# A hybrid decoder layer: an SSM norm's scaling as four jobs, with new places for sample matmuls, norm matmuls, PSUM banks and weight splits

## The chip, the cores and the metric

One core of one Trainium2 chip runs the kernel. The metric is the device time of one execution in microseconds (us), as the median of a kernel's runs.

## The reference

One decoder layer acts on 1024 prompt tokens (with 16 learned tokens ahead of them, 1040 columns) and on 8 sample tokens, so 1048 columns in the mixing part and 1032 after it. The model width is 1024, and everything is fp32.

```python
h += 0.5 * SwiGLU_1(rmsnorm(h))             # width 2816
u  = rmsnorm(h) @ w_in                      # q, f, v, g of 4 HGRN2 heads; z, x, B, C, dt of the SSM
# HGRN2, per head, chunkwise: S_t = diag(f_t) S_{t-1} + k_t v_t^T ; o_t = S_t^T q_t
#   then rmsnorm per head, times silu(u_g)
# SSM (Mamba-2): h_t = exp(dt_t A) h_{t-1} + dt_t x_t B_t^T ; y_t = h_t C_t + D x_t
#   then y * silu(z), rmsnorm over each of 2 groups of 256
h += concat(hgrn_out, ssm_out) @ w_out
h += 0.5 * SwiGLU_2(rmsnorm(h))
y  = rmsnorm(h)                             # the states are outputs too
```

Each of the 8 sample tokens has a state of its own for every head: the state is read, updated by one step, written out, and multiplied with the token's q.

## The kernel before

**Layout.** Activations lie transposed: a tile holds 128 features by all columns. A product has fp32 accuracy by three matmuls of rounded parts (`mm3`, L163 to L165: high by high, high by low, low by high). These three lines hold most of the program; a triple of them on 128 features and one column range is called a k-step here. Splitting a tile into the two parts takes one copy on ACT and one subtraction on DVE (L462 and L466 for FFN weights, L346 and L352 for FFN operands, L157 and L158 for w_in and w_out).

**PSUM.** Four banks ("mis", `K.psm()`) serve small things, and four ("acc") serve the wide products: two pairs in the FFNs (`K.psum2()`), and four single banks elsewhere (`K.psum()`). `K.banks(n)` closes and reopens the acc pool; `down` calls it ahead of its last product.

**FFNs.** Each runs seven products in place of eight per block of four weight tiles, in the manner of Strassen; the numbers 1 to 7 name them. `Blocks` makes the operands of one column half (`scaled` is ACT L335, `sum_` is DVE L341, `cast` is ACT L346, `low` is DVE L352), `Left` the weights (`sum_`, then `split` = `hi` L462 and `lo` L466). `pair` computes a gate and up tile and evacuates each product in `post`: 1 by an ACT copy L674, 6 by DVE L676 (which needs the copy), 2 by ACT L678, 5 by DVE L683 (which needs L676), 7 by L685. `first2` lists the order of the second FFN's first pair, whose operands are made while its first products run: `before(S, n, ...)` puts work ahead of step n. In an FFN the order of PE, DVE, ACT and SP is this written one. `down` ends an FFN; its evacuation is DVE L932.

**The mixing part.** The four HGRN2 heads run one after another (`hgrn_scan`). A head goes through levels m = 1, 2, 4, ..., 64 with small matmuls (L1767, and L1758 for m = 32 and 64), then transposes, chunk states (L1835), outputs (L1854 to L1861) and, last, the output of the 8 sample tokens, L1864: the 128x128 state against one column of q. Between these come the wide w_in products: `fill(n)` issues n k-steps, and every `fill.period`-th k-step pops one entry of the list `fill.jobs`. `samples` updates four states at a time (L1717 on ACT, L1718 on DVE) in levels 2 and 16. In this part only PE's order is the written one; ACT, DVE and SP are ordered by a scheduler with a cost model.

**Norms.** `ssm_norm` squares and sums, forms 1 / rms and multiplies two tiles of 128x1032 by it (L1625); group 0 runs after head 0, with z0 projected, group 1 at the end of the part. `hgrn_out` normalizes a head: ACT squares (L1875), a matmul against ones sums over partitions (L1890, head 3 only), `rstd_wide` makes 1 / rms (L194 to L204), DVE multiplies (L1881). Head 3's `hgrn_out` and all of `out_proj` stand after the written order and are ordered by the scheduler on every engine. `out_proj` runs four times: part 1 on column half 0 is the pass whose `after2` feeds the second FFN's norm `nf2` (squares on ACT L229, sums on POOL L230, the matmul L237, and so on). Its DVE addition of a bank to h is L1912.

## Time and profile before

| what | value |
|---|---|
| three runs | 1952.58, 1956.12, 1958.87 us; median 1956.12 |
| the profiled execution's own time | 1959.24 us |
| its span, first to last instruction | 1957.5 us |
| mean granted clock of TensorE | 0.993 |
| DMA | 260.59 MB, mean 133 GB/s |

The profile is of one execution; the 1.74 us between its time and its span lie around the program. Engines are PE (TensorE), DVE (VectorE), ACT (ScalarE), POOL (GpSimd) and SP. A row of a table by windows gives a stretch in us from the span's start, its length, the busy time and number of instructions of each engine, the granted clock of PE as a share of full speed, the busy share of the DMA engines and GB/s. A row of a timeline gives start, length, engine, line, operation, tiles and shape, and in brackets the idle time ahead of it with what ended it. fp32 matmuls appear in the trace as two records each.

### The profile page before, as it was taken

How to read it: one execution, taken by the hardware profiler on the slowest of the kernel's cores; microseconds unless marked ns; L12 is line 12 of the kernel's file. 1: busy time of each engine (PE TensorE's matmuls, PEld its weight loads, DVE VectorE, ACT ScalarE, POOL GpSimd, SP SyncE). 2: the span in 40 equal slices, each digit the busy share in tenths (PEclk: the TensorE clock that was granted, in tenths of full speed). 3: DMA queues.
4: the chain of work that ended last, by engine and by line, in shares of the span. 5: the costliest groups of instructions: out<-in, count | busy, mean ns of one | idle time of the engine just before them, and what ended most of it. 6: DMA issues, size and time to landing. Idle time of an engine off the chain costs nothing.

```text
span 1957.5 us, 41043 instructions
## 1 busy us (share of the span) xinstructions
PE 1917.1 (98%) x16569; PEld 1883.5 (96%) x16569; DVE 1532.7 (78%) x2783; ACT 850.3 (43%) x1632; POOL 91.5 (5%) x155
## 2 busy tenths in 40 slices
PE   7999999999999999999999999999999999999997
PEld 6999999999999999999999999999999999999997
DVE  7788888888788867576765657888888888878965
ACT  7533233333533644466644535742332323354353
POOL 4000000000000410000000001200000000000000
PEclk9999999999999999999999999999999999999999
DMA  7223333335977551221641454224332333587862
GB/s 222 77 88 109 93 99 105 100 97 161 283 234 251 158 159 51 66 87 44 177 122 52 124 172 135 77 82 120 92 109 87 103 104 104 161 245 233 271 194 77
DMA packets 324646, 260.59 MB, mean 133 GB/s; under 512 B 17824, under 2 KB 299680, under 8 KB 324448
## 3 DMA queue, kind: packets, MB, share of 16 engines
q1 hardware_dynamic: 324216, 257.92, 43.5%
q8 instruction: 131, 2.15, 0.5%
q14 instruction: 59, 0.48, 0.1%
q0 software_dynamic: 224, 0.04, 0.0%
q10 hardware_dynamic: 16, 0.00, 0.0%
HBM read 192.90 MB, written 65.07 MB: 132 GB/s over the span
## 4 chain that ended last, share of the span: by engine, by line
PE 86%; DVE 7%; DMA 2%; ACT 2%; issue 1%; SPq 0%; POOL 0%; DVEq 0%; ACTq 0%; POOLq 0%
PE acc L163 26%; PE acc L165 25%; PE acc L164 25%; PE mis L163 1%; PE mis L165 1%; PE mis L164 1%; DVE u L352 1%; DVE ws L466 1%; DMA s<-in_x_prompt_dram 1%; DMA r<-in_w_ffn_up_dram 1%; DVE r L458 1%; PE mis L1767 1%; DMA s<-cumd 1%; PE mis L1835 0%; DVE t L669 0%
## 5 line engine op out<-in xcount | busy, mean ns | idle before, releaser
L163 PE MATMUL acc<-u,ws 128*128 128x258 f32 (+3 forms) x4248 | 1243.1, 293 | 7.5 <-DVE t L683 2.5
L164 PE MATMUL acc<-u,ws 128*128 128x258 f32 (+3 forms) x4248 | 1233.2, 290 | 4.4 <-DVE u L352 4.0
L165 PE MATMUL acc<-u,ws 128*128 128x258 f32 (+3 forms) x4248 | 1232.6, 290 | 3.3 <-DVE ws L466 3.3
L163 PEld LDWEIGHTS acc<-u,ws 128*128 128x128 f32 x4248 | 805.1, 190 | 12.9 <-issue 3.6
L164 PEld LDWEIGHTS acc<-u,ws 128*128 128x128 f32 x4248 | 807.5, 190 | 6.9 <-DVE u L352 5.0
L165 PEld LDWEIGHTS acc<-u,ws 128*128 128x128 f32 x4248 | 804.9, 189 | 4.7 <-DVE ws L466 4.6
L466 DVE TENSOR_TENSOR ws<-r,ws 128x512 fp32r<-128x512 f32 x276 | 190.9, 693 | 75.0 <-ACT ws L462 74.9
L462 ACT CAST ws<-r 128x512 fp32r<-128x512 f32 x276 | 160.1, 615 | 12.9 <-ACT ws L462 7.7
L458 DVE TENSOR_TENSOR r<-r,r 128x512 f32<-128x512 f32 x176 | 120.9, 689 | 4.8 <-DMA r<-in_w_ffn_up_dram 3.3
L681 ACT ACTIVATE t<-t 128x516 f32<-128x516 f32 (+1 forms) x41 | 26.2, 639 | 213.3 <-DVE t L669 213.3
L712 ACT ACTIVATE t<-t 128x524 f32<-128x524 f32 (+1 forms) x47 | 29.9, 639 | 196.3 <-DVE t L669 196.3
L846 DVE TENSOR_TENSOR u<-u,u 128x1048 fp32r<-128x1048 f32 (+3 forms) x84 | 97.0, 1157 | 5.5 <-ACT u L842 5.5
L669 DVE TENSOR_TENSOR t<-t,u 128x524 f32<-128x524 f32 (+1 forms) x135 | 92.9, 697 | 2.9
L158 DVE TENSOR_TENSOR ws<-r,ws 128x512 fp32r<-128x512 f32 x88 | 60.6, 699 | 42.2 <-ACT ws L157 41.9
L230 POOL TENSOR_TENSOR t<-t,t 128x262 f32<-128x262 f32 (+1 forms) x56 | 54.4, 982 | 812.5 <-ACT t L229 708.5
L903 ACT CAST ws<-u 128x512 fp32r<-128x512 f32 (+1 forms) x72 | 42.2, 586 | 102.2 <-DVE u L898 92.1
L842 ACT CAST u<-u 128x1048 fp32r<-128x1048 f32 (+3 forms) x84 | 82.9, 989 | 0.0
L932 DVE SCALAR_TENSOR_TENSOR s<-acc,s 128x524 f32<-128x524 f32 (+3 forms) x88 | 54.6, 643 | 31.7 <-PE acc L165 31.4
L903 ACT CAST ws<-r 128x512 fp32r<-128x512 f32 (+1 forms) x84 | 47.9, 582 | 70.8 <-DVE r L898 29.5
L908 DVE TENSOR_TENSOR ws<-r,ws 128x512 fp32r<-128x512 f32 (+1 forms) x84 | 57.4, 693 | 23.2 <-ACT ws L903 23.1
L157 ACT CAST ws<-r 128x512 fp32r<-128x512 f32 x88 | 53.9, 617 | 36.5 <-PE acc L165 30.6
L908 DVE TENSOR_TENSOR ws<-u,ws 128x512 fp32r<-128x512 f32 (+1 forms) x72 | 47.4, 658 | 26.5 <-ACT ws L903 26.5
(435 smaller groups left out, 2290.7 us busy)
## 6 DMA issues: line engine op xcount, KB each, us to landing
r<-in_w_ffn_down_dram SPq DMA_DIRECT2D x128, 256.0 KB
hd<-s SPq DMA_DIRECT2D x93, 258.0 KB
r<-in_w_ffn_gate_dram SPq DMA_DIRECT2D x88, 256.0 KB
r<-in_w_ffn_up_dram SPq DMA_DIRECT2D x88, 256.0 KB
hd<-s SPq DMA_DIRECT2D x77, 262.0 KB
u<-hd SPq DMA_DIRECT2D x36, 516.0 KB
u<-hd SPq DMA_DIRECT2D x28, 524.0 KB
r<-in_w_in_dram SPq DMA_DIRECT2D x56, 256.0 KB
```

What stands on the lines that cost most here:

```text
L158: self.nc.vector.tensor_sub(lo, src, hi.bitcast(F32))
L163: mm(ps, whi, xhi, start=first, stop=False, skip_group_check=more)
L164: mm(ps, whi, xlo, start=False, stop=False, skip_group_check=more)
L165: mm(ps, wlo, xhi, start=False, stop=last, skip_group_check=more)
L458: self.K.nc.vector.tensor_tensor(self.raw[p], self.raw[x], self.raw[y], op)
L462: self.K.nc.scalar.copy(self.w[p][:, : self.n * P], self.raw[p])
L466: self.K.nc.vector.tensor_sub(t[:, 512 : 512 + w], self.raw[p], t[:, :w].bitcast(F32))
L669: nc.vector.tensor_mul(t, t if src is None else src, spread.lanes(i, cs))
L842: K.nc.scalar.copy(hi, lo.bitcast(F32))
L846: K.nc.vector.tensor_sub(lo, lo.bitcast(F32), hi.bitcast(F32))
L903: nc.scalar.copy(w[p, j, g][:, : n * P], src)
L908: nc.vector.tensor_sub(t[:, 512 : 512 + n * P], box[0], t[:, : n * P].bitcast(F32))
```

## The change

1. **SSM norm.** `ssm_norm` returns its two multiplications as four functions of half a row each (128x516). Group 0's become entries of `fill.jobs`, with the spills of the two tiles as entries behind them; group 1's run at once.
2. **Sample outputs.** `hgrn_scan` issues the 8 matmuls of the sample tokens in two groups of four, in levels m = 32 and m = 64, each group into a mis bank of its own, which an ACT copy empties into a small SBUF tile `os8`. The last piece of a head's output, 24 columns before, becomes 16 columns in PSUM and 8 in `os8`.
3. **Head 3's norm.** `hgrn_out` takes mis banks for its sums, not acc banks.
4. **The norm of the second FFN, half 0.** Two `nf2.end(q)` at the end of `out_proj`'s part 1 become one `begin_half(0)` and one `finish` within the next pass.
5. **`down`.** The first block of the last product takes a mis bank.
6. **`first2`.** The products' order 1, 5, 2, 6, 7, 3, 4 becomes 1, 5, 6, 2, 7, 3, 4; the splits of weights 7 and 3 move from ahead of the first step into steps 1 to 3; `scaled` can be issued in pieces of its four rows.

```diff
-    def scaled(self, h, wcol, ps):
+    def scaled(self, h, wcol, ps, ks=range(4)):
...
-            t = self.new(p)
-            for k in range(4):
+            t = self.new(p) if 0 in ks else self.b[p]
+            for k in ks:
...
-                                box.append(K.psum()[:, :K.Q])
+                                box.append((K.psum() if c or j else K.psm())[:, :K.Q])
...
-    for i, y in enumerate((ya, yb)):
-        nc.vector.scalar_tensor_tensor(y, y, K.pc["ssm_norm"][:, 2 * g + i : 2 * g + i + 1], r, ALU.mult, ALU.mult)
+    def scale(i, cs):
+        y = (ya, yb)[i][:, cs]
+        nc.vector.scalar_tensor_tensor(y, y, K.pc["ssm_norm"][:, 2 * g + i : 2 * g + i + 1], r[:, cs], ALU.mult, ALU.mult)
+
+    return [lambda i=i, cs=cs: scale(i, cs) for i in range(2) for cs in (slice(0, TO // 2), slice(TO // 2, TO))]
...
+    os8 = small("os8", P, NS)
+
+    def outputs(b0):
+        ps = K.psm()
+        for i in range(4):
+            nc.tensor.matmul(ps[:, i : i + 1], states[b0][:, i], qs[:, b0 + i : b0 + i + 1], start=True, stop=True)
+        nc.scalar.copy(os8[:, b0 : b0 + 4], ps[:, 0:4])
...
+        if m >= 32:
+            outputs({32: 0, 64: 4}[m])
...
-    for b in range(NS):
-        nc.tensor.matmul(po8[:, 16 + b : 17 + b], states[b // 4 * 4][:, b % 4], qs[:, b : b + 1], start=True, stop=True)
-    pieces.append((po8, 1024 - NM, 24))
+    pieces.append((po8, 1024 - NM, 16))
+    pieces.append((os8, TP - NM, NS))
...
-            pr = K.psum()
+            pr = K.psm()
...
-                ssm_norm(K, 0, "s", fill)
-                for i in range(2):
-                    spill(2 + i, K.y[i][:, NM:])
+                while fill.jobs:
+                    fill.jobs.pop(0)()
+                a0, b0, a1, b1 = ssm_norm(K, 0, "s", fill)
+                fill.jobs += [a0, b0, lambda: spill(2, K.y[0][:, NM:]), a1, b1, lambda: spill(3, K.y[1][:, NM:])]
...
-        ssm_norm(K, 1, "s", fill)
+        for fn in ssm_norm(K, 1, "s", fill):
+            fn()
...
-        if k == KT - 1 and q < 2:
-            nf2.end(q)
-            if q == 1:
-                keep2(0)
+        if (k, q) == (KT - 1, 1):
+            keep2(0)
+
+    def norm2(k, q):
+        if (k, q) == (0, 3):
+            nf2.begin_half(0)
+        elif (k, q) == (1, 2):
+            nf2.finish((0, 0))
...
-    out_proj(K, a, h, 0, opa, 1)
+    out_proj(K, a, h, 0, opa, 1, norm2)
...
+        w.split(6)
+        e.low(5)
+        e.scaled(h, wn2, (2,), (0, 1))
         w.split(2)
-        e.low(5)
-        w.split(6)
-        w.split(7)
-        w.split(3)
-        before(S, 1, (e.scaled, h, wn2, (2,)))
-        before(S, 2, (e.scaled, h, wn2, (3,)), (e.cast, 2))
-        before(S, 3, (e.sum_, 6), (e.low, 2), (nf2.begin_half, 1))
+        e.scaled(h, wn2, (2,), (2,))
+        before(S, 1, (e.scaled, h, wn2, (2,), (3,)), (w.hi, 7), (e.scaled, h, wn2, (3,), (0, 1)), (w.lo, 7))
+        before(S, 2, (w.hi, 3), (e.scaled, h, wn2, (3,), (2, 3)), (e.cast, 2))
+        before(S, 3, (w.lo, 3), (e.sum_, 6), (e.low, 2), (nf2.begin_half, 1))
...
-        return 1, 5, 2, 6, 7, 3, 4
+        return 1, 5, 6, 2, 7, 3, 4
```

The line numbers of the new program differ: its L1754 is the sample output, L1769 stands for L1758 of before, L1902 for L1890, L1893 for L1881, L1626 for L1625, L1924 for L1912.

**PE, head 0.** Before, the eight sample outputs (L1864, the states in two raw tiles r) end the head, behind the last prompt outputs and ahead of the wide products (ws are weights, u operands):

```order
L1854 MATMUL mis_11472<-s_10924,s_10878 128x128
L1856 MATMUL mis_11472<-s_10876,s_11422 128x128
L1860 MATMUL mis_11481<-p_1381_10926,vt_1372_10879 128x16
L1861 MATMUL mis_11481<-s_10876,s_11422 128x16
L1864 MATMUL mis_11481<-qs_10900,r_10963 128x1 x4
L1864 MATMUL mis_11481<-qs_10900,r_11135 128x1 x4
L163 MATMUL acc_11418<-u_8463,ws_11163 128x344
L164 MATMUL acc_11418<-u_8471,ws_11163 128x344
```

Now, the same four-matmul groups at level 64, the second group, with wide products on both sides (the first group stands likewise at level 32):

```order
L163 MATMUL acc_11290<-u_8463,ws_10855 128x350
L164 MATMUL acc_11290<-u_8471,ws_10855 128x350
L165 MATMUL acc_11290<-u_8463,ws_10855 128x350
L1769 MATMUL mis_11346<-s_10876,u_10026 64x64 x8
L1754 MATMUL mis_11356<-qs_10900,r_11136 128x1 x4
L163 MATMUL acc_11367<-u_8456,ws_10850 128x348
L164 MATMUL acc_11367<-u_8464,ws_10850 128x348
L165 MATMUL acc_11367<-u_8456,ws_10850 128x348
```

The end of the head has lost its tail of one-column matmuls, and levels 32 and 64 have gained four each.

**PE, head 3's norm.** Before, the three sums of `hgrn_out` (L1890) stand together after the last w_in product and ahead of `out_proj`'s first matmul:

```order
L165 MATMUL acc_14165<-u_8463,ws_13508 128x344
L1890 MATMUL acc_14224<-u_14216,ones_83 128x496
L1890 MATMUL acc_14227<-u_14216,ones_83 128x512
L1890 MATMUL acc_14230<-u_14216,ones_83 128x24
L163 MATMUL acc_14268<-u_13567,ws_14260 128x258
L164 MATMUL acc_14268<-u_13568,ws_14260 128x258
```

Now 27 matmuls of `out_proj` (from acc_14303 on) stand ahead of the first of four sums, and others between them:

```order
L163 MATMUL acc_14331<-u_13590,ws_14295 128x258
L164 MATMUL acc_14331<-u_13591,ws_14295 128x258
L165 MATMUL acc_14331<-u_13590,ws_14295 128x258
L1902 MATMUL mis_14256<-u_14246,ones_83 128x496
L163 MATMUL acc_14331<-u_13832,ws_14295 128x258
L164 MATMUL acc_14331<-u_13833,ws_14295 128x258
L165 MATMUL acc_14331<-u_13832,ws_14295 128x258
L163 MATMUL acc_14331<-u_14020,ws_14300 128x258
L1902 MATMUL mis_14259<-u_14246,ones_83 128x512
L1902 MATMUL mis_14262<-u_14246,ones_83 128x16
L164 MATMUL acc_14331<-u_14021,ws_14300 128x258
L165 MATMUL acc_14331<-u_14020,ws_14300 128x258
```

The sums moved into the stream of `out_proj`, and they write mis banks.

**DVE, the same place.** Now the scaling of the second SSM norm (L1626) and the rest of its 1 / rms (L203, L204) stand between `out_proj`'s first addition and the second (L1924), where before the first three additions stood together behind them:

```order
L1924 TENSOR_TENSOR s_14277<-s_14277,acc_14303 128x258
L203 SCALAR_TENSOR_TENSOR s_14158<-s_14158,s_14159 128x1032
L1893 SCALAR_TENSOR_TENSOR u_14091<-mis_14138,col,u_14091 128x496
L204 SCALAR_TENSOR_TENSOR s_14159<-s_14158,s_14159 128x1032
L1893 SCALAR_TENSOR_TENSOR u_14091<-mis_14146,col,u_14091 128x512
L1626 SCALAR_TENSOR_TENSOR u_9184<-u_9184,col,s_14159 128x516 x2
L1626 SCALAR_TENSOR_TENSOR u_9404<-u_9404,col,s_14159 128x516 x2
L1893 SCALAR_TENSOR_TENSOR u_14091<-mis_14155,col,u_14091 128x16
L1893 SCALAR_TENSOR_TENSOR u_14091<-os_1696_13645,col,u_14091 128x8
L1924 TENSOR_TENSOR s_14277<-s_14277,acc_14317 128x258
```

So the second addition now has two rows of 1032 columns, two of about 500, four of 516 and two short ones ahead of it (L1893 is the multiplication that was L1881).

**DVE, the second FFN's first pair.** Before, from the split of weights 7 and 3 (the last two L466) on:

```order
L466 TENSOR_TENSOR ws_15570<-r_15470,ws_15570 128x512
L466 TENSOR_TENSOR ws_15573<-r_15536,ws_15573 128x512
L341 TENSOR_TENSOR u_15630<-u_15609,u_15556 128x1032
L352 TENSOR_TENSOR u_15632<-u_15591,u_15614 128x1032
L676 TENSOR_TENSOR t_15660<-acc_15647,t_15589 128x258
L683 TENSOR_TENSOR t_15662<-acc_15596,t_15660 128x258
L341 TENSOR_TENSOR u_15549<-u_15609,u_15549 128x1032
L685 TENSOR_TENSOR t_15684<-mis_15671,t_15662 128x258
L352 TENSOR_TENSOR u_15686<-u_15630,u_15664 128x1032
```

Now:

```order
L466 TENSOR_TENSOR ws_15618<-r_15498,ws_15618 128x512
L676 TENSOR_TENSOR t_15656<-acc_15643,t_15615 128x258
L683 TENSOR_TENSOR t_15658<-acc_15624,t_15656 128x258
L466 TENSOR_TENSOR ws_15637<-r_15564,ws_15637 128x512
L341 TENSOR_TENSOR u_15661<-u_15620,u_15584 128x1032
L352 TENSOR_TENSOR u_15663<-u_15595,u_15641 128x1032
L341 TENSOR_TENSOR u_15577<-u_15620,u_15577 128x1032
L685 TENSOR_TENSOR t_15712<-mis_15699,t_15658 128x258
L352 TENSOR_TENSOR u_15714<-u_15661,u_15692 128x1032
```

The evacuation of products 6 and 5 (L676, L683) stands ahead of two operand steps (L341, L352) and one split, where it stood behind them.

4 lines of the change are left out of this document (2 added, 2 removed).

## The prediction

> **What bounds the kernel.** I read first the page's busy times and the shares of the chain of work that ended last.
>
> ```profile
> PE 1917.1 (98%) x16569; PEld 1883.5 (96%) x16569; DVE 1532.7 (78%) x2783; ACT 850.3 (43%) x1632; POOL 91.5 (5%) x155
> PE 86%; DVE 7%; DMA 2%; ACT 2%; issue 1%; SPq 0%; POOL 0%; DVEq 0%; ACTq 0%; POOLq 0%
> ```
>
> PE is busy 1917.1 of 1957.5 us. The change adds one matmul and removes none worth counting, so it can gain only in two places: the 40.4 us in which PE waits, and stretches in which PE counts as busy but runs slowly. For the first, the waits of PE by line:
>
> ```profile
> PE acc L1890 <- ACT u L1875: 2.9, 1, 2.9
> ```
>
> It is the longest one that the change touches; the others come with their parts. For the second, windows of 3.4 us around the sample outputs (L1864), with the granted clock as the third number from the end:
>
> ```profile
> 961.00:964.40 3.40, 3.40 (x31) 3.25 (x29) 3.40 (x18) 2.87 (x9) 0.27 (x3) 1.00 0.15 46
> 964.40:967.80 3.40, 3.40 (x13) 3.40 (x13) 3.40 (x12) 2.20 (x6) 0.00 (x0) 0.51 1.02 272
> 1053.20:1056.60 3.40, 3.40 (x31) 3.25 (x29) 1.48 (x2) 0.84 (x2) 0.99 (x2) 1.00 0.00 0
> 1056.60:1060.00 3.40, 3.40 (x24) 3.40 (x25) 2.65 (x4) 0.47 (x4) 0.12 (x1) 1.00 0.02 5
> 1104.40:1107.80 3.40, 3.40 (x29) 3.25 (x29) 1.02 (x2) 0.88 (x5) 1.24 (x3) 1.00 0.98 340
> 1107.80:1111.20 3.40, 3.40 (x14) 3.40 (x13) 3.38 (x4) 1.43 (x4) 0.00 (x0) 0.50 0.12 49
> 1159.00:1162.40 3.40, 3.40 (x31) 3.25 (x30) 0.00 (x0) 0.00 (x0) 0.00 (x0) 1.00 0.77 233
> 1162.40:1165.80 3.40, 3.40 (x14) 3.40 (x14) 0.00 (x0) 0.46 (x1) 0.00 (x0) 0.50 1.01 399
> ```
>
> In three of four heads the window behind the sample outputs runs at half clock, and PE does 13 or 14 instructions where it does 24 in the one undisturbed window (1056.60). That PE is full in the window ahead doesn't prevent it. [...]
>
> **The change, part by part.** All sums go against the profiled run's own 1959.24 us; 1.74 us of it lie around the span. It is 3.1 us above the median of the three runs; I come back to that.
>
> *Sample outputs (T).* The group of one head in the chain of work; wide matmuls behind it at half clock, in the timeline; and one at full clock, in the chain:
>
> ```profile
> 1160.90 1.88 PE mis L1864 x16
> ...
> 1166.22 0.16 PE acc L163
> ```
>
> ```profile
> 1163.94 0.49 PE L164 MATMUL acc<-u,ws 128*128 128x344 f32 x1
> 1164.22 0.49 PE L165 MATMUL acc<-u,ws 128*128 128x344 f32 x1
> ```
>
> At half clock a wide matmul starts every 0.28 to 0.29 us, at full clock every 0.16, so 3.4 us at half clock cost 3.4 x (1 - 0.16 / 0.29) = 1.52 us; with the unrounded spacings, 0.157 and 0.287, it is 1.55. At full clock 344 columns in 0.157 us are 2.2 columns per ns, which I use to estimate how much of a window streams. The 16 records of a group carry one column each, so their 1.88 us stream nothing. The rest of such a window, 1.5 us, holds these:
>
> ```profile
> 1104.01 0.39 PE L1854 MATMUL mis<-s,s 128*128 128x128 f32 x2
> 1104.23 0.39 PE L1856 MATMUL mis<-s,s 128*128 128x128 f32 x2
> ```
>
> Two records of 128 columns every 0.22 us are 0.12 us of streaming, half, so the window streams about 0.8 us at most. After the change four of the eight outputs stand at level 32 and four at level 64. What stands at level 64 now, and the update of the sample states that ends closest ahead of it:
>
> ```profile
> 1089.82 1.15 PE L1758 MATMUL mis<-s,u 128*64 128x64 f32 x16
> 1086.59 0.59 DVE L1718 SCALAR_TENSOR_TENSOR r<-r,qs,r 128x128 f32<-128x128 f32 x2
> ```
>
> A window at level 64 will hold these 1.15 us (16 x 64 columns, 0.47 us of streaming), 0.94 us of sample outputs (none) and 1.3 us of wide products, nearly all streaming: about 1.7 us, an estimate. That is twice what stands ahead of the halved windows, so I take it that the clock stays. The instructions themselves only move, at 0. The states are ready at 1087.2, and the new place is 1091.0: 3.8 us of slack, so no wait. Two more ACT copies per head lie on an engine that is 43% busy. **T = 3 x 1.55 = -4.65.** Its bounds: 0 (the windows stay) and -4.65.
>
> *The bank in `down` (B).*
>
> ```profile
> 681.39 0.36 PE L163 MATMUL acc<-u,ws 128*128 128x262 f32 x1 [0.89 <-DVE s L932]
> 1909.18 0.36 PE L163 MATMUL acc<-u,ws 128*128 128x258 f32 x1 [0.88 <-DVE s L932]
> ```
>
> These are the first matmuls behind the reopened pool, which wait for the last evacuation of the old one. The new block's bank is another pool's, long free, so its 11 k-steps (33 matmuls at some 0.12 us) cover the 0.9 us. **B = -1.77.** Bounds 0 and -1.77.
>
> *Head 3's norm (H).* The chain ahead of its sums:
>
> ```profile
> 1171.82 1.28 ACT L194
> ...
> 1177.28 0.50 ACT u L1875
> 1177.82 1.26 PE acc L1890 x4
> ```
>
> PE stood idle for 2.9 us of it, since the sums held its queue. Now 27 matmuls of `out_proj` come first, at 0.12 us each in this stretch, which gives
>
> ```profile
> 1179.29 0.12 PE acc L164
> ```
>
> 27 x 0.12 = 3.2 us of cover. What is late next: DVE. Its second `out_proj` addition now stands behind four half-row multiplications and the rest of the SSM norm's 1 / rms. Full rows of the same multiplication cost
>
> ```profile
> 1020.08 2.49 DVE L1625 SCALAR_TENSOR_TENSOR u<-u,col,s 128x1032 f32<-128x1032 f32 x2
> ```
>
> 1.25 us, so the ten rows are worth some 2.5 + 2.5 + 1.2 + 0.1 = 6.3 us, while the four acc banks hold 48 matmuls, 48 x 0.12 = 5.8 us. The fifth group can wait for a bank, by what DVE started late. From 0 to the whole 2.9; I take half, **H = -1.5**.
>
> *The second FFN's norm (E).*
>
> ```profile
> 1225.74 0.70 PE L237 MATMUL mis<-t,ones 128*128 128x258 f32 x2 [0.58 <-POOL t L230]
> 1229.18 0.70 PE L237 MATMUL mis<-t,ones 128*128 128x258 f32 x2 [0.22 <-POOL t L230]
> ```
>
> Both sums now stand 24 matmuls of the next pass later, 24 x 0.12 = 2.9 us of cover against 0.6. **E = -0.8**, bounds 0 and -0.8.
>
> *`first2` (A).* PE's waits in its first pair, and the windows around them (the order is PE, PEld, DVE, ACT, POOL):
>
> ```profile
> 1276.94 0.39 PE L163 MATMUL acc<-u,ws 128*128 128x258 f32 x1 [0.54 <-ACT t L674]
> 1283.44 0.39 PE L163 MATMUL acc<-u,ws 128*128 128x258 f32 x1 [1.03 <-DVE t L683]
> 1288.89 0.39 PE L163 MATMUL acc<-u,ws 128*128 128x258 f32 x1 [0.87 <-ACT t L674]
> ```
>
> ```profile
> 1256.00:1278.10 22.10, 21.56 (x179) 21.36 (x179) 22.07 (x31) 16.46 (x38) 13.67 (x14) 1.00 0.30 96
> 1278.10:1280.10 2.00, 2.00 (x16) 1.89 (x15) 0.00 (x0) 2.00 (x7) 0.00 (x0) 1.00 1.05 378
> 1280.10:1293.10 13.00, 11.10 (x91) 10.69 (x90) 12.51 (x18) 8.38 (x14) 0.00 (x0) 1.00 0.07 25
> ```
>
> The three waits are 2.44 us. DVE is full before 1278.1, idle for 2.0 us (ACT is making operands), and full again until 1293: the first pair is bound by DVE's row of operand steps, and DVE's sum of work does not shrink. What the new order gives back is that idle hole, with a split and two evacuations moved into it. I take half of the waits, **A = -1.2**; bounds 0 and -2.44.
>
> *The SSM norm's four jobs (C).* DVE's two multiplications of group 0 lie at 1020.08 to 1022.57 (above), and PE stands still for another reason at the same time:
>
> ```profile
> 1019.64 0.49 PE L1767 MATMUL mis<-s,u 128*32 128x16 f32 x35
> 1021.89 0.40 PE L1767 MATMUL mis<-s,u 128*32 128x16 f32 x27 [1.76 <-issue]
> 1019.10:1022.50 3.40, 1.64 (x71) 1.30 (x70) 2.74 (x4) 1.20 (x4) 0.00 (x0) 1.00 0.91 238
> 1022.50:1025.90 3.40, 3.40 (x13) 3.40 (x13) 3.06 (x11) 3.12 (x10) 0.00 (x0) 0.50 1.10 373
> ```
>
> Nothing that the profile shows released PE at 1021.89; the DMA engines are 0.91 busy in the window, and I suspect that PE's next instructions came late behind them, which no view proves. The window's 62 records of 16 columns (0.45 us at 2.2 per ns) and the few wide ones beside them stream about 1.1 us, and the clock halves behind it, as behind the sample outputs. So the pieces, which let DVE serve the level's steps between them, free nothing while that stall stands: **C = 0**. [...]
>
> **Sum:** -4.65 - 1.77 - 1.5 - 0.8 - 1.2 = -9.9, so 1959.24 - 9.9 = 1949.3. The median run is 3.1 us shorter than the profiled one. If it had two half-clock windows fewer (2 x 1.55), it ends at the same 1949.3. If it had one fewer and saved the other 1.55 us elsewhere, two are left to lose, and 1956.12 - 3.1 - 5.27 = 1947.8 (5.27 is the sum without T). I forecast the middle, **1948.5**.
>
> [...]
>
> **Rivals.**
> 1. *The clock answers to idle time alone.* Then PE, full at 1159.00 to 1162.40, isn't what halves it, the windows have another cause and stay: T = 0, and 1948.5 + 3.9 = 1952.4 (4.65 from one anchor, 3.1 from the other). For it: head 1 has the same outputs (1053.20) without a fall. Against it: three falls, each right behind them. Chance 0.12. [...]
> 2. *DVE stays the bound at both FFN2's start and `out_proj`.* H and A give 0: 1948.5 + 2.7 = 1951.2. For it: DVE 22.07 of 22.10. Against it: the hole of 2.0 us that DVE has at 1278.1. Chance 0.18.
> 3. *The stall at 1020 goes too,* as the stream of instructions shifts: -1.76, and -1.55 for the half-clock window behind it: 1945.2. Against it: nothing in the change aims at it. Chance 0.2.
> 4. *Slower: the new places throttle.* Levels 32 and 64 of four heads are eight windows with fewer columns. If the clock falls below about 1.7 us of streaming rather than 1.1 (the point from which this case decides), each costs 1.55: 1948.5 + 8 x 1.55 = 1960.9. That is slower than before's 1956.12. Against it: behind the level at 1089.82 the next fall comes only at 1107.80. Chance 0.05.
>
> **How the numbers follow.** Forecast (within about 2 us) 0.45. The range goes from rival 3 with A and H at their upper bounds (1945.2 - 1.7) to rival 1 with a part of rival 2: 1943.5 to 1953.5; some 0.15 is left out. A measurement of this kernel can tell about 0.3% from no change, here 5.9 us: faster means below 1950.3, slower above 1962.0. Of the forecast 0.43 lies below, of rival 3 all 0.20, of rival 2 some 0.07 and of rival 1 some 0.02: faster 0.72. Rival 4 lies at the edge of slower, with 0.03 above it: slower 0.03, and the rest, 0.25, is no change that can be told.
>
> **What would show it.** T: granted clock 1.00 in every window of the four heads but the one behind 1020, and no L1754 group ahead of a halved window. B: no wait of L163 for the line L932 at the start of the last product. H: no idle time ahead of L1902 and at most 1.5 us at the fifth group behind the new L1924. E: no wait for L230. A: two of the three waits in the first pair halved and DVE's hole near 1279 filled. It would be wrong if half-clock windows show at levels 32 or 64, or if DVE's evacuations hold PE longer in `out_proj` than 2.9 us.

## The result, and the profile after

| | before | after |
|---|---|---|
| median of 10 runs | 1956.31 us (1952.15 to 1960.04) | 1951.57 us (1948.45 to 1953.69) |
| ratio | | 0.9973, 95% interval 0.9962 to 0.9984 |
| the profiled execution's own time | 1959.24 us | 1949.43 us |

The change is worth 4.7 us, 0.27%: faster, since the interval leaves 1 out, but just under the 0.3% that the prediction had called the limit. By that limit (1950.3) it is "no change that can be told", to which the prediction had given 0.25, not the "faster" of 0.72. The two profiled executions are 9.8 us apart, twice as much; so a part of what they show is chance of the one run, and has to be told from the change. The busy times and the waits of PE after, from the page and from the view of waits (total, times, longest):

```profile
PE 1913.8 (98%) x16571; PEld 1882.3 (97%) x16571; DVE 1533.1 (79%) x2789; ACT 850.3 (44%) x1642; POOL 91.9 (5%) x155
```

```profile
PE mis L1778 <- issue: 2.4, 3, 1.0
PE acc L165 <- DVE ws L466: 2.2, 4, 0.8
PE acc L163 <- DVE t L683: 2.2, 1, 2.2
PE acc L164 <- DVE u L352: 2.1, 3, 0.9
PE acc L163 <- DVE s L1924: 1.9, 2, 1.0
...
PE acc L163 <- issue: 1.2, 1, 1.2
```

The wait for ACT's squares ahead of head 3's sums (2.9 us) and the two for L932 (1.8 us) are gone. New ones are two for L1924, one of 2.2 us for L683, and more waits without a releaser. The start of each wide matmul in the two traces, matched by number, gives the difference stretch by stretch:

| stretch | before, us | after minus before, us |
|---|---|---|
| start, to about 150 us | 137.2 | -2.7 |
| the rest of the first FFN | 521.0 | -0.1 |
| start of its last product (B) | 18.2 | -1.2 |
| projections and SSM ahead of the heads | 222.0 | -2.0 |
| the four heads (T, C) | 255.4 | -4.3 |
| head 3's norm, first out_proj groups (H) | 27.2 | +0.3 |
| the next passes of out_proj (E) | 57.3 | -1.3 |
| the second FFN's first pair (A) | 55.4 | -0.05 |
| the rest of the second FFN | 597.1 | +2.5 |
| start of its last product (B) | 11.6 | -1.1 |

The start and the projections differ by as much among all profiles of this study, parts of the change or not; those 4.7 us are chance (the profiled run of before has the longest start of all). What is left, -5.2 us, is about the measured gain. The windows after (busy times of PE, PEld, DVE, ACT and POOL; then PE's clock, DMA share, GB/s), at level 64 of heads 0 and 2 with the window behind each, then in the first pair of the second FFN:

```profile
941.50:944.90 3.40, 3.40 (x33) 3.11 (x32) 3.20 (x16) 2.41 (x10) 0.00 (x0) 1.00 0.45 120
944.90:948.30 3.40, 3.40 (x27) 3.37 (x26) 0.99 (x3) 1.05 (x3) 0.00 (x0) 1.00 0.72 213
1081.50:1084.90 3.40, 3.40 (x33) 3.11 (x33) 2.25 (x6) 2.25 (x8) 0.00 (x0) 1.00 0.51 144
1084.90:1088.30 3.40, 3.40 (x25) 3.36 (x25) 1.04 (x3) 1.63 (x6) 0.00 (x0) 1.00 0.00 0
1279.40:1282.80 3.40, 1.39 (x11) 1.42 (x12) 3.37 (x5) 0.18 (x1) 0.00 (x0) 1.00 0.00 0
1282.80:1286.20 3.40, 3.40 (x18) 3.40 (x17) 3.37 (x8) 0.62 (x1) 0.00 (x0) 0.51 0.27 77
```

No window in the heads is halved any more, as forecast; but one behind the new wait for L683 is, which before had not. And out_proj's two waits, in the timelines of PE and of DVE:

```profile
1179.51 0.39 PE L163 MATMUL acc<-u,ws 128*128 128x258 f32 x1 [0.98 <-DVE s L1924]
...
1180.99 0.39 PE L163 MATMUL acc<-u,ws 128*128 128x258 f32 x1 [0.96 <-DVE s L1924]
```

```profile
1166.14 0.42 DVE L1924 TENSOR_TENSOR s<-s,acc 128x258 f32<-128x258 f32 x1
...
1170.07 2.75 DVE L1626 SCALAR_TENSOR_TENSOR u<-u,col,s 128x516 f32<-128x516 f32 x4
1172.74 0.22 DVE L1893 SCALAR_TENSOR_TENSOR u<-mis,col,u 128x16 f32<-128x16 f32 x1
1172.88 0.21 DVE L1893 SCALAR_TENSOR_TENSOR u<-os,col,u 128x8 f32<-128x8 f32 x1
1173.02 1.08 DVE L1924 TENSOR_TENSOR s<-s,acc 128x258 f32<-128x258 f32 x3
```

DVE's second addition starts 6.9 us behind its first, near the 6.3 us that the prediction had counted, and four acc banks (5.8 us) don't reach that far.

### The profile page after: what moved, and what is told of

It reads as the page before. It is cut to its first block, busy times and chain, and to the rows that moved or that the text cites. A ratio compares the mean times of both kernels' runs of the same rounds, so it can differ in the third digit from the quotient of the medians.

```text
span 1947.7 us, 41061 instructions
## 1 busy us (share of the span) xinstructions
PE 1913.8 (98%) x16571; PEld 1882.3 (97%) x16571; DVE 1533.1 (79%) x2789; ACT 850.3 (44%) x1642; POOL 91.9 (5%) x155
## 4 chain that ended last, share of the span: by engine, by line
PE 88%; DVE 7%; DMA 2%; ACT 2%; issue 1%; SPq 0%; DVEq 0%; POOL 0%; ACTq 0%; POOLq 0%
PE acc L163 26%; PE acc L165 26%; PE acc L164 25%; PE mis L163 2%; PE mis L165 2%; PE mis L164 2%; DVE u L352 1%; DVE u L341 1%; DVE u L846 1%; DVE ws L466 1%; PE mis L1452 0%; DMA s<-nr 0%; PE mis L1848 0%; PE mis L1778 0%; PE mis L1448 0%
## 5 line engine op out<-in xcount | busy, mean ns | idle before, releaser
L163 PE MATMUL acc<-u,ws 128*128 128x258 f32 (+4 forms) x4226 | 1235.1, 293 | 7.1 <-DVE t L683 2.2
L164 PE MATMUL acc<-u,ws 128*128 128x258 f32 (+4 forms) x4226 | 1224.6, 290 | 3.9 <-DVE u L352 2.1
L165 PE MATMUL acc<-u,ws 128*128 128x258 f32 (+4 forms) x4226 | 1225.4, 290 | 2.3 <-DVE ws L466 2.2
L466 DVE TENSOR_TENSOR ws<-r,ws 128x512 fp32r<-128x512 f32 x276 | 190.3, 690 | 75.2 <-ACT ws L462 75.0
L932 DVE SCALAR_TENSOR_TENSOR s<-acc,s 128x524 f32<-128x524 f32 (+3 forms) x86 | 53.8, 648 | 29.8 <-PE acc L165 29.5
```

The costliest lines, as they stand in the source:

```text
L163: mm(ps, whi, xhi, start=first, stop=False, skip_group_check=more)
L164: mm(ps, whi, xlo, start=False, stop=False, skip_group_check=more)
L165: mm(ps, wlo, xhi, start=False, stop=last, skip_group_check=more)
L466: self.K.nc.vector.tensor_sub(t[:, 512 : 512 + w], self.raw[p], t[:, :w].bitcast(F32))
```

## The experiments

A further quantity is used here: each run has its mean granted clock. In the profiles of before and after the clock is 1.00 or 0.50 throughout. In before it is 0.50 in the last 6.55 us, where PE does nothing, and in six stretches of 3.41 us, from 18.95, 763.06, 964.45, 1022.47, 1107.81 and 1162.42 us: their starts lie 218, 59, 17, 25 and 16 times that length apart, and a window is a piece of this grid. Together that is 27.0 us, which (1 - clock) x 2 x span gives too; for the other runs this product is taken as the time at half clock. Over 95 runs of before, the mean time is 1956.7 us (standard error 0.3) and the mean half-clock time 23.5 us (0.6). Some 5.5 us of that lie at the very end of the span, behind the last wide matmul (4.1 to 6.6 us in the 14 profiles); the other 18 us are about five windows of 3.4 us in a mean run. Below, "mean" is a mean of runs with its standard error, and a ratio is against runs of before taken beside the experiment. Those beside experiments 9 to 12 have a mean of 1955.8 us (0.6), those beside 1 to 8 of 1956.9 and 1957.0 (0.5 each), so a comparison of means across these groups can be off by 1 us.

### 1. The sample outputs alone

The kernel before with the second item of the change and no other.

```diff
+        if m >= 32:
+            outputs({32: 0, 64: 4}[m])
...
-    for b in range(NS):
-        nc.tensor.matmul(po8[:, 16 + b : 17 + b], states[b // 4 * 4][:, b % 4], qs[:, b : b + 1], start=True, stop=True)
```

> The kernel before with the sample outputs alone moved into levels 32 and 64 (a quarter of them each, per head and group of four); the other five parts stay as before. Streaming theory (the clock halves behind a window of 3.4 us in which few columns stream, however full PE is): no half-clock window between 930 and 1170 us apart from one behind a stall without a releaser; the time falls by what before loses there, up to 3 x 1.55 = 4.65 us, so 1951.7 to 1953.5 against 1956.3. Rival (the clock answers to idle time alone, or the windows have another cause): halved windows stay, 1956.3 within 1 us. A second rival: the windows go, but PE's waits without a releaser (1.9 us in the profile before, 4.2 us in the profile after, between 920 and 1125 us) grow by some 2.3 us for the moved instructions, and the time falls by 2 to 2.5 us only.

Measured: median 1956.66, ratio 0.9995 (0.9983 to 1.0008). Mean 1956.6 (0.5), mean half-clock time 19.9 us (1.3). The four heads took 5.8 us less in the profile, and no window there is halved; yet the time is that of before. So the part on which nearly half of the forecast rested (4.65 of 9.9 us) shows no gain in the time. Experiment 9 follows where it went.

### 2. The change without the moved sample outputs

The same item undone.

```diff
-        if m >= 32:
-            outputs({32: 0, 64: 4}[m])
...
+    for b in range(NS):
+        nc.tensor.matmul(po8[:, 16 + b : 17 + b], states[b // 4 * 4][:, b % 4], qs[:, b : b + 1], start=True, stop=True)
```

> The changed kernel with the sample outputs back at the end of each head. Streaming theory: two to three of the four heads have a half-clock window behind the 16 one-column records again, +3.1 to +4.65 us on 1951.6, so 1954.7 to 1956.2. Rival (idle time alone): 1951.6. Second rival (moved instructions lengthen the waits without a releaser): windows come back, those waits shrink to about 2 us, and the time is 1953 to 1954.

Measured: median 1950.97, ratio 0.9977 (0.9966 to 0.9987), half-clock time 21.6 us (1.4). The halved windows are back behind three of the four heads, and the time is that of the whole change. Experiments 1 and 2 agree from both sides.

### 3. The change without the new first pair

```diff
-        return 1, 5, 6, 2, 7, 3, 4
+        return 1, 5, 2, 6, 7, 3, 4
...
```

(and the splits back ahead of the first step)

> The changed kernel with the old first pair of the second FFN (products 1, 5, 2, 6, 7, 3, 4 and weights 7 and 3 split ahead). In the profile after, the new first pair has one wait of 2.2 us for L683 at 1281 us and a half-clock window behind it (1.5 us), against 3.6 us lost in short waits before. Theory (DVE's row of work is the bound there, and the new order only gathers the waits in one place, which then also halves the clock): three short waits again, no half-clock window near 1283, and a time of 1950 to 1951.6. Rival (the new order gains the 1.2 us that were forecast): 1952.8 or more.

Measured: median 1951.21, ratio 0.998 (0.9968 to 0.9993), mean 1952.3 (0.8) against 1951.2 (0.5) of the whole change. Time can't tell these apart; the waits of PE from 1250 to 1300 us can, first without the new pair, then with it:

```profile
PE acc L163 <- ACT t L674: 1.7, 2, 0.9
PE acc L163 <- DVE t L683: 1.0, 1, 1.0
PE acc L165 <- DVE ws L466: 0.2, 1, 0.2
```

```profile
PE acc L163 <- DVE t L683: 2.2, 1, 2.2
```

2.9 us of short waits become one of 2.2 us, which in 7 of the 8 profiles with the new pair is followed by a half-clock window of 1.5 us. The stretch takes 0.3 us more without the new pair than before's, and 0.05 us less with it: a saving of some 0.4 us. Seven of the eight profiles with the new pair agree with that within 0.05 us; in the eighth (experiment 4), where no window is halved behind the wait, it is 1.0 us.

### 4. All eight sample outputs at level 64

```diff
-        if m >= 32:
-            outputs({32: 0, 64: 4}[m])
+        if m == 64:
+            outputs(0)
+            outputs(4)
```

> The changed kernel with all eight sample outputs of a head at level 64, right behind its 16 matmuls of 64 columns; same instructions. Streaming theory: 1.15 us of 64-column matmuls (0.47 us of streaming) and 1.88 us of one-column matmuls nearly fill a window, which streams 0.8 us; the clock halves behind level 64 in two to four of the four heads, though PE is full there: +3.1 to +6.2 us on 1951.6. Rival (the point lies lower, or it is the end of the head that matters): no halved window, 1951.6.

Measured: median 1952.26, ratio 0.9973 (0.9962 to 0.9985): the same as the change, and no halved window in a head. The expectation of 0.8 us of streaming took for granted that a window falls just onto both groups of small matmuls. In the profile three of the four heads split them between two windows; in the fourth all 16 records lie in one, with wide matmuls (L1754's share of the window first, then the window and the next):

```profile
1083.40:1086.90 3.50, 1.95 (x16) 1.86 (x16) 1.00 0.12 36
```

```profile
1083.40:1086.90 3.50, 3.50 (x30) 3.43 (x28) 1.42 (x5) 1.43 (x5) 0.00 (x0) 1.00 0.12 36
1086.90:1090.30 3.40, 3.40 (x26) 3.36 (x25) 0.91 (x3) 2.33 (x7) 0.00 (x0) 1.00 0.02 5
```

Behind 1.95 us of one-column matmuls with 1.5 us of wide ones the clock stayed at 1.00 (1086.90). Counted by columns, no window with these records streamed less than about 1.6 us (3,484 columns at the prediction's 2.2 per ns); the test of a lower value didn't take place.

### 5 to 7. The place of the operand tiles

The profiles of experiments 1 to 4 showed something else: the spacing of wide matmuls differs between kernels with the tile `os8` and without it, in both FFNs, and repeats within 0.06 ns in the profiles of kernels that agree in this tile. `os8` takes 32 bytes per partition, and all s and u tiles that are allocated behind it lie 32 bytes further.

```diff
# 5: before, and in hgrn_scan
+    nc.gpsimd.memset(small("pad8", P, NS), 0.0)
# 6 and 7: the change, with
-    os8 = small("os8", P, NS)
+    os8 = small("os8", P, 16)[:, :NS]        # 7: 24
```

> The kernel before with one more small tile of 8 floats (32 bytes per partition, cleared once per head), allocated where the change has its tile for the sample outputs; nothing else. In the profiles so far the mean spacing of the wide matmuls is 121.86 ns in the first FFN and 119.81 to 119.87 ns in the second without that tile, 121.54 and 120.23 to 120.25 ns with it. Address theory (the operand tiles that are allocated behind it lie 32 bytes further, and that sets the spacing): 121.54 and 120.24 ns here too, so about -1.6 us over some 5,100 matmuls of the first FFN and +2.0 us over some 5,200 of the second, +0.4 us in sum, within the noise of the time. Rival (the spacing has to do with the moved matmuls or with the run): 121.86 and 119.84 ns.

> The changed kernel with the sample outputs' tile 16 floats wide instead of 8 (64 bytes), 8 of them unused; nothing else. Address theory, if it is the place modulo 64 bytes that counts: the spacing of before, 121.86 and 119.84 ns, so +1.6 and -2.0 us, 1951.2 in the median. If more than 64 bytes count: a third pair of values. Rival (the tile's place is without effect): 121.54 and 120.24 ns as in the changed kernel.

> The changed kernel with that tile 24 floats wide (96 bytes). Address theory modulo 64 bytes: as the changed kernel, 121.54 and 120.24 ns. If more than 64 bytes count, a fourth pair. Rival without effect of the place: the same 121.54 and 120.24 ns, so that this run speaks only together with the one of 16 floats.

Two stretches without waits, 330 us of the first FFN and 380 us of the second; the number to read is that behind PE's busy time, the matmuls done in it. Before, after, and experiments 5, 6 and 7:

```profile
150.00:480.00 330.00, 330.00 (x2710) 330.00 (x2709) 283.48 (x482) 103.56 (x191) 0.00 (x0) 1.00 0.36 109
1320.00:1700.00 380.00, 380.00 (x3167) 379.42 (x3166) 327.81 (x555) 115.44 (x215) 0.00 (x0) 1.00 0.35 103
```

```profile
150.00:480.00 330.00, 330.00 (x2717) 330.00 (x2716) 286.05 (x486) 105.91 (x195) 0.00 (x0) 1.00 0.36 110
1320.00:1700.00 380.00, 380.00 (x3158) 379.78 (x3157) 328.51 (x557) 118.79 (x219) 0.00 (x0) 1.00 0.35 105
```

```profile
150.00:480.00 330.00, 330.00 (x2717) 330.00 (x2717) 284.90 (x484) 105.36 (x194) 0.00 (x0) 1.00 0.36 110
1320.00:1700.00 380.00, 380.00 (x3157) 379.61 (x3156) 326.14 (x553) 115.52 (x216) 0.00 (x0) 1.00 0.35 103
```

```profile
150.00:480.00 330.00, 330.00 (x2710) 330.00 (x2709) 283.60 (x482) 103.84 (x192) 0.00 (x0) 1.00 0.36 109
1320.00:1700.00 380.00, 380.00 (x3161) 379.79 (x3160) 327.07 (x555) 118.83 (x221) 0.00 (x0) 1.00 0.35 105
```

```profile
150.00:480.00 330.00, 330.00 (x2715) 330.00 (x2714) 284.23 (x483) 104.57 (x193) 0.00 (x0) 1.00 0.36 110
1320.00:1700.00 380.00, 380.00 (x3162) 379.36 (x3161) 326.85 (x554) 118.30 (x220) 0.00 (x0) 1.00 0.35 104
```

A tile of 32 bytes that does nothing makes the first FFN faster by 7 matmuls in 330 us and the second slower by 10 in 380, just as in the changed kernel. As mean spacings (the gaps of waits left out): 121.86 and 119.87 ns before, 121.54 and 120.23 after, 121.54 and 120.25 with the empty tile, 121.85 and 120.17 with 64 bytes, 121.61 and 119.98 with 96. The place modulo 64 bytes doesn't account for it: 64 bytes leave it as in before, and the second FFN has 120.17 ns against 119.87. The times (ratios 1.0002, 0.9982 and 0.9975, each within 0.0015) can't show differences of this size: by the spacings the 32 bytes cost -1.6 us over some 5,100 matmuls and +2.0 us over some 5,200, an estimate. In the profile of experiment 5 the first FFN, from 150 us on, took 1.1 us less than in that of before, and the second, behind its first pair, 1.8 us more.

### 8. B and E alone

The kernel before with items 4 and 5 of the change.

```diff
-                                box.append(K.psum()[:, :K.Q])
+                                box.append((K.psum() if c or j else K.psm())[:, :K.Q])
...
-    out_proj(K, a, h, 0, opa, 1)
+    out_proj(K, a, h, 0, opa, 1, norm2)
```

> The kernel before with two parts of the change only: the mis bank for the first block of down's last product, and the norm of the second FFN's half 0 within the next pass. By the profiles after, these two give -1.0 us at each down and -1.3 us at the norm: -3.3 us, so 1953.3 on the mean of before, 1956.9 (35 runs, standard error 0.5). If the other parts carry more than half of the measured gain of 5 us, this kernel shows less than 2.5 us, 1954.5 or more.

Measured: median 1953.00, ratio 0.9982 (0.9968 to 0.9996); mean 1953.2 (1.0), that is -3.5 us (1.1). The two stretches of `down` and that of `out_proj` took 1.1, 1.1 and 1.3 us less in the profile. So about two thirds of the gain (-3.5 of -5.5 us between the means, with an error of 1.1) come from these two small edits.

### 9. The sample outputs alone, without a new address

```diff
-    os8 = small("os8", P, NS)
+    os8 = fp.tile([P, NS])
```

(on the kernel of experiment 1; the columns lie in a free corner of a tile that exists)

> The kernel before with the sample outputs alone moved into levels 32 and 64, as in the first experiment, but their 8 columns lie in a free corner of a tile that exists already, so that no operand tile moves: spacings of 121.86 and 119.84 ns as before. Theory (the moved outputs save about one half-clock window per run on the mean, since others halve elsewhere, above all at head 3's norm, where PE stands idle for 2.9 us; the address cost 0.4 us): 1956.97 - 1.6 to 1956.97 - 0.5, so 1955.4 to 1956.5 on the mean, mean half-clock time 20 us against 24.0 us of 70 runs of before. If the address shift alone had eaten the gain of three windows: 1952.3 to 1953.5.

Measured: median 1956.29, ratio 1.0005 (0.9993 to 1.0017); mean 1956.2 (0.6), half-clock time 19.5 us (1.1); spacings as before. So it wasn't the address. Both kernels with the moved outputs alone (23 runs): 1956.4 (0.4) against 1956.7 (0.3), and half-clock time 19.7 (0.8) against 23.5 (0.6) us: 1.1 windows fewer, not three. In both their profiles the heads are clean, and the next weak place is hit, head 3's sums. The timeline of PE, and ACT's, of this kernel; then ACT's of before:

```profile
1171.68 1.99 PE L1899 MATMUL acc<-u,ones 128*128 128x496 f32 x2 [3.26 <-ACT u L1884]
```

```profile
1169.40 1.28 ACT L1641 ACT_TABLE_LOAD   x1
1170.70 0.46 ACT L1641 ACTIVATE u<-acc 128x344 f32<-128x344 f32 x1
1171.05 1.15 ACT L1884 ACTIVATE u<-mis 128x496 f32<-128x496 f32 x3
```

```profile
1170.77 0.60 ACT L1875 ACTIVATE u<-mis 128x496 f32<-128x496 f32 x1
1171.24 0.57 ACT L1622 ACTIVATE s<-acc,eps 128x344 f32<-128x344 f32 x1
1171.82 1.28 ACT L194 ACT_TABLE_LOAD   x1
```

```profile
1168.30:1171.70 3.40, 0.14 (x2) 0.02 (x1) 2.25 (x2) 3.37 (x6) 0.00 (x0) 1.00 0.00 0
1171.80:1175.20 3.40, 3.40 (x5) 1.39 (x6) 3.40 (x5) 2.17 (x6) 0.00 (x0) 0.51 0.16 27
```

Two things happened there. The scheduler, with four pieces in place of three, put the first square behind both table loads, so that the first sum (1.0 us, at 1173.94 before) no longer fits ahead of the wait. And the wait of 3.3 us lies in one window, so the four sums behind it run at half clock. Together the stretch takes 2.2 us (experiment 1) and 2.3 us (this one) longer than in the profile before.

The second of these doesn't need the moved outputs. In experiment 8, with ACT's order of before and the same wait of 2.89 us, 2.4 us of the wait fall into one window, the clock halves behind it, and the stretch takes 2.9 us longer. In the profile before the wait is split between two windows, 1.1 and 1.7 us, and the clock stays. The windows of experiment 8, then those of before:

```profile
1164.70:1168.10 3.40, 1.02 (x4) 0.22 (x2) 1.74 (x2) 3.37 (x6) 0.00 (x0) 1.00 0.00 0
1168.10:1171.50 3.40, 2.90 (x7) 1.86 (x8) 3.40 (x5) 2.39 (x6) 0.00 (x0) 0.50 0.02 5
```

```profile
1172.66:1176.07 3.41, 2.27 (x12) 1.47 (x10) 0.53 (x1) 3.38 (x6) 0.00 (x0) 1.00 0.00 0
1176.07:1179.48 3.41, 1.66 (x8) 1.19 (x9) 3.38 (x4) 3.34 (x7) 0.00 (x0) 1.00 0.03 5
```

So one wait of 2.89 us had a half-clock window behind it in one profile and none in the other, and the difference seen there is how it lay on the windows.

### 10. The second SSM norm's multiplications behind out_proj's first pass

```diff
-        for fn in ssm_norm(K, 1, "s", fill):
-            fn()
+        scales = ssm_norm(K, 1, "s", fill)
...
     out_proj(K, a, h, 0, opa, 0)
+    for fn in scales:
+        fn()
```

(on the change, with the 96-byte tile of experiment 7)

> The changed kernel with the second SSM norm's four half-row multiplications run behind the first pass of out_proj instead of ahead of it, and the sample outputs' tile 24 floats wide (the spacings of that run: 121.61 and 119.98 ns, worth -0.9 us against the changed kernel). Theory (in the changed kernel the two waits of 1.1 us at 1179 and 1181 us are acc banks that DVE empties late, behind those multiplications, and they make a window with few columns): both waits go or fall under 0.5 us, no half-clock window at 1181 to 1185, so -2.2 to -3.8 us in that stretch and with the spacing 1947 to 1949. Rival (DVE is late there by its other rows too, two of 1032 columns and two of about 500): one wait of about 1 us stays, 1949.5 to 1951.

Measured: median 1947.12 of 8 runs (1946.00 to 1953.57), ratio 0.9969 (0.9954 to 0.9984); mean 1948.6 (1.1). It is the lowest median of the kernels that compute all, on few runs: its interval overlaps that of the change. Five of the eight runs lie at 1946.0 to 1947.9 us, and the profiled one (1952.31) is one of the three others. PE's only wait from 1165 to 1215 us:

```profile
PE acc L165 <- DVE ws L158: 1.2, 1, 1.2
```

Both waits for banks are gone, no window is halved there, and the stretch took 2.6 us less than before's, where the change took 0.3 us more. The new wait is for a weight's split that DVE does later, at 1194.46, and with it the next passes took 1.6 us more than in the change. So the four multiplications were what made the banks late, and their work has to be done somewhere: of the 2.9 us between the two kernels in this stretch, 1.3 us are left behind the next passes.

### 11. Without the sample states' transfers

```diff
-        nc.sync.dma_start(sb, a["state_hgrn"][0, b0 : b0 + 4, hd].rearrange("b k v -> k b v"))
-        nc.sync.dma_start(vb, vd[b0 : b0 + 4].partition_broadcast(P))
+        nc.gpsimd.memset(sb, 0.0)
+        nc.gpsimd.memset(vb, 0.0)
...
-        nc.sync.dma_start(o["hgrn_sample"][0, b0 : b0 + 4, hd].rearrange("b k v -> k b v"), sb)
```

> The changed kernel without the loads of the sample states and of the rows beside them, which are cleared instead, and without the store of the new sample states: it leaves the HGRN2 sample states and what follows from them out. PE's order is the same. In ten profiles the waits without a releaser between 905 and 1160 us lose 2.3 to 5.7 us in sum. Theory (PE's own instructions come late there because their transfer stands behind data transfers): without this traffic (some 1,000 to 2,000 packets within 2 us of such a fetch) the sum falls under 1 us, -3 us on 1951.2. Rival (the queue of instructions runs dry because the small matmuls go through it too fast, whatever the data does): 3 to 5 us again.

Measured: median 1946.84 of 4 runs, ratio 0.9954 (0.9936 to 0.9972). The wait without a releaser from 905 to 1160 us, which was 2.4 + 1.2 us in four places after:

```profile
PE mis L1777 <- issue: 1.5, 1, 1.5
```

Three of four places are gone; the one near 1014 us, behind the SSM norm's own transfers of 516 KB each, stays. The place near 1122 us speaks for the traffic: all 13 other profiles have a wait there (0.2 to 1.4 us, between 1120 and 1131 us), and this one has none. The waits near 927 and 1024 us are missing in some kernels with the traffic too (before has none at 927), so one profile doesn't show a cause for them, and that the wait is for PE's instructions stays a guess. The sum, 1.5 us, lies below that of the 13 other profiles (1.7 to 4.9 us by the view of waits), but not far below the lowest. The expectation of under 1 us in sum was too low, and why the last one lasts 1.5 us, with the DMA engines idle at that moment (share 0.00 from 1012.00 to 1014.20 us), isn't settled.

### 12. The change without the first SSM norm's four jobs

Item 1 of the change undone; the second SSM norm's multiplications, too, run in whole rows again.

```diff
-                a0, b0, a1, b1 = ssm_norm(K, 0, "s", fill)
-                fill.jobs += [a0, b0, lambda: spill(2, K.y[0][:, NM:]), a1, b1, lambda: spill(3, K.y[1][:, NM:])]
+                ssm_norm(K, 0, "s", fill)
+                for i in range(2):
+                    spill(2 + i, K.y[i][:, NM:])
```

> The changed kernel with the first SSM norm's two multiplications of 1032 columns back in one piece at once, and the spills behind them. Theory of the prediction (the pieces free nothing while PE waits for another reason at that place): the same, 1951.2 within 0.9 us. Rival (the pieces keep DVE in time for the levels of head 1): a wait of PE for L1809 of 0.5 to 1.4 us near 1016 to 1026 us that the changed kernel doesn't have, 1952 to 1952.6.

Measured: median 1950.51, ratio 0.9969 (0.9957 to 0.998), mean 1950.3 (0.6) against 1951.2 (0.5). No new wait for DVE in the levels of head 1; the two rows stand at 1010.70 us, beside a wait without a releaser that ends at 1012.11. The four jobs that gave the change its name show no gain.

## Why the prediction was right, and where its steps were wrong

The forecast, 1948.5, had the direction; the measured 1951.57 lies in its range, 3.1 us above it, at the time of rival 2 (1951.2). That is in part luck: the largest term shows next to nothing, H has the wrong sign, and B and E together gave 1 us more than forecast, in a range 10 us wide. (Its lower end is a slip as well: with A and H at their upper bounds 2.6 us go off 1945.2, not 1.7.) The terms, as the experiments give them:

| term | forecast | measured | by |
|---|---|---|---|
| T, sample outputs | -4.65 (-3.1 from the median) | -0.3 (0.5) | 23 runs against 95 |
| B, the bank in `down` | -1.77 | -1.2 and -1.1 | stretches of ten profiles (-1.0 to -1.2) |
| E, the second FFN's norm | -0.8 | -1.3 | stretches of nine profiles (-1.0 to -1.4); with B -3.5 (1.1) by time |
| H, head 3's norm | -1.5 | +0.3 in the profile after | stretch; -0.5 to +1.8 in eight profiles |
| A, `first2` | -1.2 | -0.4 | stretch with and without |
| C, the four jobs | 0 | 0 (within 0.9) | experiment 12 |

These add up to -4.0 us, against -5.5 (0.6) between the means of the change and of before. What the other 1.5 us are isn't shown; the errors are not much smaller.

**The step that failed is T = 3 x 1.55.** Its mechanism, that the moved outputs clear the heads of halved windows, is right: no window in a head's levels or end is halved in any profile with them. Two things were wrong in the term. First, three windows were the count of one profiled run: of the four profiles with the outputs at the end, three have three halved heads, and one (experiment 8) none. Second, the cleared heads did not stay a gain, with the next weak place behind them: in both profiles with the outputs alone moved, head 3's sums took 2.2 us longer (a place that can halve without them, as experiment 8 shows), and in each of the nine profiles of the change and its variants a wait for L1924 or L683 is followed by a halved window. The half-clock time of the change is 23.0 us (1.5) in its ten runs, that of before 23.5 (0.6). Kernels that differ from the change only in the width of `os8` have 17.2 (1.5) and 24.4 (1.6), so this figure doesn't show a gain by the clock. The outputs alone have 3.7 us (1.1) less of it, worth some 1.7 us at 1.55 per window, of which the time shows 0.3 (0.5); why not more isn't settled. The prediction's own alternative, a median run with one or two half-clock windows fewer than the profiled one, was closer (the profiled run has 27.0 us of half clock, a mean run 23.5: one window), and should have set the term.

**Streaming as the measure**, by which the prediction took the clock to stay at the new places, was the author's estimate, and the runs don't show it. Shares of the one-column records (L1864; L1867 in experiment 2) in windows at a head's end of before, of experiment 2 and of experiment 8:

```profile
961.00:964.40 3.40, 1.85 (x16) 1.87 (x16) 1.00 0.15 46
1053.20:1056.60 3.40, 1.50 (x14) 1.53 (x14) 1.00 0.00 0
```

```profile
1101.55:1104.95 3.40, 1.59 (x15) 1.62 (x15) 1.00 0.95 316
1159.58:1162.99 3.41, 1.75 (x16) 1.66 (x15) 1.00 0.93 305
```

```profile
956.50:959.90 3.40, 1.05 (x10) 1.08 (x10) 1.00 0.30 99
```

These three profiles and that of experiment 5 have 16 ends of heads. In nine of them 15 or 16 such records start in one window, and half clock follows all nine; in the other seven the fullest window starts 9 to 14, and half clock follows none (of the 16 at 1159.58 two started in the window before). Columns don't separate the two: 1,486 start at 1053.20, not halved, against 2,144 in a window that is (experiment 2, 958.20). Nor does the time of the one-column records: 1.59 us at 1101.55 are followed by half clock, 1.75 us at 1159.58, with wide matmuls behind them, and 1.95 us in experiment 4, between wide ones, are not. No single count explains all, and the rule stays open.

For waits the profiles say more. Between 700 us and the last 13 us of the span, 13 windows in the 14 profiles have PE idle for 1.9 us or more, and half clock follows all of them (2.0 us idle at 1279.40 of after, with the wait of 2.2 us before 1281.41, and 0.51 behind it); of 37 with 1.0 to 1.8 us idle it follows three (one at 1019.10 of before, 1.76 us). Idle time alone doesn't account for the falls either: the clock also fell behind windows that were full (PE 3.40 of 3.40 us at 961.00 of before, 0.51 behind it).

**H** failed where the prediction had put the doubt: DVE 6.9 us between its additions against 5.8 us of banks, so 1.9 us of waits for the 2.9 us removed, and a halved window behind them in four of the eight profiles that have the second SSM norm's multiplications there; experiment 10 shows the cause. **A** is the prediction's own counter-argument: DVE's sum of work is the same (1532.7 us in the whole span before, 1533.1 after), its hole shrank only from 2.06 us (ahead of 1280.14) to 1.31 us (ahead of 1267.43 after), and PE's waits moved into one. **B** came out a little above the wait, and **E** gave 1.3 us where the two waits were 0.8. The first matmul behind a wait also lasts longer (0.36 us at 681.39 and 1909.18 of before, against 0.28), which would explain it, but no run tests that. **C**'s 0 was right, and its reason fits, a stall of another cause at the same place. That the sample states' transfers are this cause doesn't fit: in experiment 11 the stall near 1014 us stays without them.

**The rivals.** Rival 1 (idle time alone) gave 1952.4, near the time too, but not for its reason: the heads' windows did go. Rival 2 gave the measured time and is right that H gives nothing, and A little; but it kept T whole, so its time is a coincidence. Rival 3 didn't come: waits without a releaser from 905 to 1160 us lose 1.7 to 4.9 us in all profiles with the sample states' transfers, 1.9 in before and 3.5 in after. Rival 4 didn't: no window at levels 32 or 64 is halved.

## What to carry to other kernels

One profiled run is one draw: read what varies (half-clock windows, waits without a releaser) from several profiles, or from the mean clock of all runs, before it becomes a term with a count. Where the gain comes from a clock that was halved, look for the next place with a long wait behind it: with the heads cleared, a wait of 3.3 us at head 3's sums had a window at 0.51 behind it (experiment 9). A wait gathered into one piece can cost a half-clock window that the same sum in pieces didn't: in the second FFN's first pair one wait of 2.2 us had such a window behind it in seven of eight profiles, and the three waits of before, 2.44 us in sum, had none. And a wait removed ahead of an engine that is itself late came back in part: H took 2.9 us away and left 1.9 us, while the waits on work that nothing else needs (B, E) gave more than all the rest, 3.5 of 5.5 us.

## What the runs showed of the hardware that was not expected

- 32 bytes more per partition ahead of the operand tiles changed the spacing of the wide matmuls in both FFNs: 121.86 to 121.54 ns with 262 columns, 119.87 to 120.25 ns with 258; 64 and 96 bytes gave other pairs. That was -1.1 us in most of the first FFN and +1.8 us in most of the second (experiment 5).
- Half clock followed all nine windows at a head's end in which 15 or 16 one-column records start, with PE 3.40 of 3.40 us busy, and none of the seven where 9 to 14 do. It also followed, in 14 profiles, all 13 windows in which PE was idle for 1.9 us or more, less than a whole window, and 3 of 37 with 1.0 to 1.8 us.
- A wait of 2.9 us was followed by half clock or not according to how it fell onto the windows: behind 2.4 us in one (experiment 8) the clock was 0.50, behind 1.1 and 1.7 us in two (before) 1.00.
- PE stood still for 0.2 to 2.0 us at a time, without a releaser in the profile, mostly in bursts of small matmuls. Without the sample states' transfers three of four such waits went, one of which all 13 other profiles have.
